# A four-layer hybrid trunk: joins of the Gated DeltaNet inverse set apart, more gates beside the norm, value products of the attention in one series, HGRN2 output transposed without TensorE

## The chip, the cores and the metric

The kernel runs on one core of a Trainium2 chip. The metric is the device time of one execution in microseconds (us), as the median of several runs. TensorE is called PE, VectorE DVE, ScalarE ACT, GpSimd POOL; SyncE (SP) issues nearly all transfers.

## The reference

Four residual layers on x of 1024 positions by D = 1024, all in fp32: HGRN2, sliding-window attention (SWA), Gated DeltaNet (GDN), HGRN2. Each is a norm with a shift and scale from a condition vector, one wide input projection, a token mixer, a product with a SiLU gate, and an output projection.

```python
x = x + gate * mixer(rmsnorm(x, g) * (1 + scale) + shift)

def hgrn2_mixer(h, w_in, w_out, onorm_g, lb):          # 8 heads of 128
    q, f_pre, i_, z = jnp.split(h @ w_in, 4, axis=-1)
    log_f = jnp.log(lb + (1.0 - lb) * jax.nn.sigmoid(f_pre))
    k = (1.0 - lb) * jax.nn.sigmoid(-f_pre)
    o = hgrn2_scan(silu(q), k, i_, log_f)              # S = diag(f) S + k v^T ; o = q S
    return (rmsnorm(o, onorm_g) * jax.nn.silu(z)) @ w_out

def swa_mixer(h, w_in, w_out, ...):                    # 16 query heads, 4 key heads of 64
    q, k, v, z = split(h @ w_in)                       # q, k: norm, then rotary
    p = softmax over the last 128 keys, with a sink per head
    return ((p @ v) * jax.nn.silu(z)) @ w_out

def gdn_mixer(h, w_in, w_out, conv_w, ...):            # 8 key heads, 16 value heads of 128
    qkv, z, a, b = split(h @ w_in)
    q, k, v = split(silu(causal_conv(qkv, conv_w)))    # 4 taps; q, k: l2norm
    # per chunk: A = beta k k^T * decay (strictly lower); X = (A + I)^-1 [v beta, k beta e^d]
    # v_new = u - w S ; o = (q e^d) S + (q k^T decay) v_new ; S = S e^dlast + k^T v_new
    return (rmsnorm(o, onorm_g) * jax.nn.silu(z)) @ w_out
```

## The kernel before

x lies feature-major, 128 features by 512 positions (a half) to a tile, in eight k blocks. The norm of a half splits its result into hhi and hlo, which together hold fp32. Weights come by SP in blocks of 256 KB (w_raw, three buffers; four k blocks by 128 columns, or two by 256), ACT splits off w_hi (L179), DVE w_lo (L180), each with four buffers. A projection column of a half is 8 k blocks by the three matmuls of mm3 (L204 to L206): hi·hi, lo·hi and hi·lo, 128 x 512 each. proj_ps, projt_ps (positions on the partitions) and outp_ps, out_ps are such products and share three banks of PSUM (two tagged proj, one ta). All else on PE is plain fp32: transposes, state products, inverses. PSUM's other tags are lev (two banks), tr, o and s (one each).

The token mixers' generators yield an estimate of how much work should come between two of their steps, and weave(...) interleaves them with the projections of the next head (or unit) in proportion to such estimates; high_priority and burst set offsets of the scheduler's priorities, tied(...) keeps a list of matmuls together behind its first, and issue_after orders an instruction behind another. A side stream of the next layers' shift and scale (ada_w, ada_acc) runs beside. The scheduler writes one instruction order for each engine from this.

- The norm: norm_stats, then norm_apply (L496), for each k block one DVE pass n_t (L504, into an SBUF tile), one ACT pass hhi (L505) and one DVE pass hlo (L506). trunk calls it for each half when the layer before has written that half. early(...) projects half 0 of the next layer beside the norm of half 1.
- HGRN2 (hgrn2, L956): 8 heads, two halves each. mix forms the intra-chunk matrix in levels j = 2, 8, 32. At j = 32 the products of L1087 go into column groups of 32 of PE's columns: per chunk of 128, 96 columns in the first, 64 in the second and 32 in the third. At a half's end the normed output (L1132, DVE, from o_ps) is transposed by PE (ot_ps, L1136, four transposes), multiplied by the gate (L1139, DVE) and, for heads 0 to 6, written to od (L1141) for the output projection; head 7 goes on in SBUF. kh_ps (L1104) are four more transposes.
- SWA (swa, L1219): for each block of 128 positions four scores, softmax, then for each of two key blocks four transposes pt_ps (L1368) and two value products pv_ps (L1374). ev_k norms and rotates k in each of four evacuations.
- GDN (gdn, L537): 8 units u. proj_kq projects k and q (conv: an ACT copy to gd_xs, three DVE passes of L650 behind the ACT pass of L648), proj_v the values, proj_z two gate columns. inverse(u) joins 32-blocks to 64 and 64 to 128 in four steps (z_ps, L811, L819 to L821, L828, L836), with copies by ACT and DVE between; scan(u) then uses it. While scan(u) runs, inverse(u + 1) and the projections listed by ZL run beside it. DVE's stream transpose of 128x512 stands at L859.

## Time and profile before

| what | value |
|---|---|
| median of 3 runs | 2690.08 us (2689.09 to 2697.81) |
| the profiled execution | 2695.95 us, its span 2694.2 us, granted clock 0.992 |
| PE busy | 2609.7 us (97%) |
| DVE busy | 2010.2 us (75%) |
| ACT busy | 1272.9 us (47%) |
| DMA | 273.29 MB |

The span runs from the first to the last instruction on the engines; the execution is 1.75 us longer. Busy PE time counts the modelled end of a matmul, so plain projection matmuls of 128x512 last 0.40 us in a row of the timeline and start every 0.23 us. The layers lie at about 62 to 640 us (HGRN2), 648 to 1122 (SWA), 1122 to 2128 (GDN) and 2128 to 2694 (HGRN2).

### The profile page before, as it was taken

Reading aid. Unit: us, or ns where it says so; the run is one execution under the profiler, and the core shown is the slowest. Engines: PE = TensorE matmul, PEld = TensorE weight load, DVE = VectorE, ACT = ScalarE, POOL = GpSimd, SP = SyncE. Lnnn points to the kernel's source line nnn. Section 1 sums busy time; section 2 is a strip of 40 time slices with the busy share of each in tenths; the row PEclk is TensorE's granted clock in tenths of the full one; section 3 lists DMA queues with packets and bytes.
Section 4 is the critical chain, followed back from the end, with each engine's and each line's share of the span. In section 5 each row is a group of like instructions: output and inputs, shape, how many; then the busy total and the mean of one; then the engine's idle time right before and its main releaser. Section 6 shows DMA issues by size and latency. Waiting matters only on the chain.

```text
span 2694.2 us, 51458 instructions
## 1 busy us (share of the span) xinstructions
PE 2609.7 (97%) x18927; PEld 2102.4 (78%) x18927; DVE 2010.2 (75%) x5619; ACT 1272.9 (47%) x3268; POOL 136.7 (5%) x352
## 2 busy tenths in 40 slices
...
GB/s 241 92 93 84 68 79 72 110 137 157 59 87 103 75 158 91 114 98 84 102 115 99 96 105 100 94 97 82 179 254 132 71 60 37 56 51 43 49 118 115
DMA packets 361490, 273.29 MB, mean 101 GB/s; under 512 B 70499, under 2 KB 294166, under 8 KB 361238
## 3 DMA queue, kind: packets, MB, share of 16 engines
...
HBM read 224.77 MB, written 45.15 MB: 100 GB/s over the span
## 4 chain that ended last, share of the span: by engine, by line
PE 71%; DVE 17%; DMA 5%; ACT 3%; issue 3%; SPq 1%; POOL 0%; DVEq 0%; ACTq 0%; POOLq 0%
PE proj_ps L206 10%; PE proj_ps L205 9%; PE proj_ps L204 9%; PE outp_ps L204 5%; PE outp_ps L205 5%; PE outp_ps L206 5%; DMA ada_w<-in_ada_w_dram 3%; PE projt_ps L204 3%; PE projt_ps L206 3%; PE projt_ps L205 3%; DVE w_lo L180 2%; DVE gd_tb L650 2%; PE pv_ps L1374 1%; DVE ada_acc L413 1%; PE w_ps L890 1%
## 5 line engine op out<-in xcount | busy, mean ns | idle before, releaser
L204 PE MATMUL proj_ps<-hhi,w_hi 128*128 128x512 f32 x1664 | 675.8, 406 | 6.1 <-ACT gd_tb L648 5.9
L206 PE MATMUL proj_ps<-hhi,w_lo 128*128 128x512 f32 x1664 | 679.9, 409 | 0.0
L205 PE MATMUL proj_ps<-hlo,w_hi 128*128 128x512 f32 x1664 | 671.2, 403 | 0.0
L204 PEld LDWEIGHTS proj_ps<-hhi,w_hi 128*128 128x128 f32 x1664 | 315.3, 190 | 59.4 <-ACT gd_tb L648 6.3
L205 PEld LDWEIGHTS proj_ps<-hlo,w_hi 128*128 128x128 f32 x1664 | 314.7, 189 | 59.0 <-issue 2.4
L206 PEld LDWEIGHTS proj_ps<-hhi,w_lo 128*128 128x128 f32 x1664 | 315.0, 189 | 56.1 <-issue 1.0
L179 ACT CAST w_hi<-w_raw 128x512 fp32r<-128x512 f32 x332 | 202.0, 611 | 303.3 <-PE proj_ps L205 188.1
L180 DVE TENSOR_TENSOR w_lo<-w_raw,w_hi 128x512 fp32r<-128x512 f32 x332 | 223.1, 674 | 155.2 <-ACT w_hi L179 129.1
L205 PE MATMUL projt_ps<-w_lo,hhi 128*128 128x256 f32 x896 | 258.7, 291 | 4.7 <-DVE w_lo L180 4.7
L204 PE MATMUL projt_ps<-w_hi,hhi 128*128 128x256 f32 x896 | 257.8, 290 | 0.6 <-ACT w_hi L179 0.6
L206 PE MATMUL projt_ps<-w_hi,hlo 128*128 128x256 f32 x896 | 256.8, 290 | 0.0
L204 PE MATMUL outp_ps<-o_hi,w_hi 128*128 128x512 f32 x576 | 229.2, 400 | 4.7 <-ACT o_hi L1200 3.4
L205 PE MATMUL outp_ps<-o_lo,w_hi 128*128 128x512 f32 x576 | 229.4, 399 | 0.0
L206 PE MATMUL outp_ps<-o_hi,w_lo 128*128 128x512 f32 x576 | 226.8, 396 | 0.7 <-DVE w_lo L183 0.7
L205 PEld LDWEIGHTS projt_ps<-w_lo,hhi 128*128 128x128 f32 x896 | 171.1, 192 | 8.1 <-DVE w_lo L180 6.0
L204 PEld LDWEIGHTS projt_ps<-w_hi,hhi 128*128 128x128 f32 x896 | 171.1, 192 | 3.7 <-ACT w_hi L179 1.0
L206 PEld LDWEIGHTS projt_ps<-w_hi,hlo 128*128 128x128 f32 x896 | 170.8, 192 | 2.4 <-issue 1.0
L650 DVE SCALAR_TENSOR_TENSOR gd_tb<-gd_xs,taps,gd_tb 128x512 f32<-128x512 f32 x192 | 145.2, 756 | 28.3 <-ACT gd_tb L648 19.7
L182 ACT ACTIVATE w_hi<-w_raw,par 128x512 fp32r<-128x512 f32 (+1 forms) x136 | 94.3, 698 | 137.0 <-PE outp_ps L205 89.2
L204 PEld LDWEIGHTS outp_ps<-o_hi,w_hi 128*128 128x128 f32 x576 | 108.8, 189 | 29.1 <-ACT o_hi L1200 4.9
L413 DVE SCALAR_TENSOR_TENSOR ada_acc<-ada_w,par,ada_acc 128x512 f32<-128x512 f32 x140 | 104.8, 749 | 33.4 <-DMA ada_w<-in_ada_w_dram 32.5
L206 PEld LDWEIGHTS outp_ps<-o_hi,w_lo 128*128 128x128 f32 x576 | 108.7, 189 | 23.5 <-DVE w_lo L183 1.3
...
## 6 DMA issues: line engine op xcount, KB each, us to landing
ada_w<-in_ada_w_dram SPq DMA_DIRECT2D x160, 256.0 KB, 2.8
w_raw<-in_hg_in_w_dram SPq DMA_DIRECT2D x136, 256.0 KB, 2.8
w_raw<-in_gd_in_w_dram SPq DMA_DIRECT2D x108, 256.0 KB, 3.0
o_in<-od SPq DMA_DIRECT2D x72, 256.0 KB, 3.2
w_raw<-in_gd_out_w_dram SPq DMA_DIRECT2D x64, 256.0 KB, 2.9
w_raw<-in_sw_in_w_dram SPq DMA_DIRECT2D x48, 256.0 KB, 2.9
w_raw<-in_hg_out_w_dram SPq DMA_DIRECT2D x40, 256.0 KB, 2.8
...
```

The lines of the kernel that those rows point to most:

```text
L179: nc.scalar.copy(hi, raw)
L180: nc.vector.tensor_tensor(lo, raw, hi.bitcast(F32), ALU.subtract)
L182: nc.scalar.activation(hi, raw, AF.Copy, scale=scale)
L204: mm(out, a[0], b[0], start=start, stop=False)
L205: mm(out, a[0], b[1], start=False, stop=False)
L206: mm(out, a[1], b[0], start=False, stop=stop)
L413: self.nc.vector.scalar_tensor_tensor(acc, w, c, acc, ALU.mult, ALU.add)
L650: nc.vector.scalar_tensor_tensor(y, xs[:, j:j + HT], w(j), y, ALU.mult, ALU.add)
L890: nc.tensor.matmul(po[:, hd[a]], dd["u"][a, hf][:, cs], rhs, start=True, stop=True)
L1374: nc.tensor.matmul(po[a * 64:(a + 1) * 64], vg[:, n + 1 - nkb + b, :], p4[:, :, a, :], start=b == 0, stop=b == nkb - 1)
```

## The change

In HGRN2, heads 0 to 6, the four PE transposes of the output go. The norm's product writes the half as blocks of 32 positions, DVE's stream transpose turns the 32x32 blocks, four DMAs of 64 KB put them into their places in a DRAM tile pd, one DMA reads the transposed half back (256 KB), and the gate product and the write to od follow at level 8 of the next half. The level-32 products become sixteen matmuls in four column groups, 64 columns in the fullest per chunk, all tied.

The norm's n_t goes to PSUM (tag lev). norm_apply is a generator, and for half 1 it is left to the next layer: HGRN2 and SWA drain it at their start; GDN drains four k blocks behind the convolution of each of its first two columns (k and q), and hold puts the next convolution's copy behind the last hhi of them.

In GDN, gates of units 1 and 2 for half 0 are projected early, beside the norm, and later gates are each done one half earlier (ZL), which loads 24 more weight blocks. The four steps of an inverse's joins are issued after the last projection matmul emitted before them (apart) and yield 2200 each. In SWA the value products of a block form one series behind all its transposes; k's evacuations go in pairs with one 16-wide rsqrt; and the order at the start is v and q for half 0 early, then v, k, z, q.

```diff
-NB = {"n_acc": 1, "n_sq": 2, "n_t": 2}
+NB = {"n_acc": 1, "n_sq": 2}
-ZL = ((2, 0, 1),), ((3, 0, 1),), ((4, 0, 1),), ((5, 0, 1),), ((6, 0),), ((6, 1),), ((7, 0, 1),), ()
+ZL = ((2, 1), (3, 0)), ((3, 1), (4, 0)), ((4, 1), (5, 0)), ((5, 1), (6, 0)), ((6, 1),), ((7, 0),), ((7, 1),), ()
...
+    def apart(self, mms):
+
+        with self.tc.issue_after(self.mm.ins):
+            self.tied(mms)
...
-        mm(out, a[1], b[0], start=False, stop=stop)
+        self.mm = mm(out, a[1], b[0], start=False, stop=stop)
...
     def norm_apply(self, i, hf, rb):
+
         nc = self.nc
...
-            t = self.np.tile([P, HT], F32, name="n_t", tag="n_t", bufs=NB["n_t"])
+            t = self.psum("lev", "n_t", 2)
             G, S = self.gcol[:, i, k:k + 1], self.shift(i, k)
             nc.vector.scalar_tensor_tensor(t, x[:, k, :], G, rb, ALU.mult, ALU.mult)
-            nc.scalar.activation(hhi[:, k, :], t, AF.Identity, bias=S)
+            self.piece = nc.scalar.activation(hhi[:, k, :], t, AF.Identity, bias=S)
             nc.vector.scalar_tensor_tensor(hlo[:, k, :], t, S, hhi[:, k, :].bitcast(F32), ALU.add, ALU.subtract)
+            yield 1
...
-            nc.scalar.copy(xs[:, 3:], ps)
+            with self.tc.issue_after(self.hold.ins) if self.hold else nullcontext():
+                nc.scalar.copy(xs[:, 3:], ps)
...
             for j in (2, 1, 0):
-                nc.vector.scalar_tensor_tensor(y, xs[:, j:j + HT], w(j), y, ALU.mult, ALU.add)
+                last = nc.vector.scalar_tensor_tensor(y, xs[:, j:j + HT], w(j), y, ALU.mult, ALU.add)
+
+            self.piece = None
+            with self.tc.issue_after(last.ins):
+                drain(take(self.last, self.parts))
+            self.hold = self.piece
...
-            yield 900
+            yield 2200
             za, zb = bank("z_ps", 32), bank("z_ps", 32)
-            self.tied([f for g in range(N) for f in (
+            self.apart([f for g in range(N) for f in (
...
-        self.early(proj_kq(0, ds[0], ((0,),)), EV)
+        self.parts = 4
+        self.early(chain(proj_kq(0, ds[0], ((0,),)), proj_z(1, ds[1], (0,)), proj_z(2, ds[2], (0,))), EV)
+        drain(self.last)
         self.spill_x(1)
         decays()
         drain(proj_kq(0, ds[0], ((1,),)))
-        weave(self.tc, (inverse(0, ds[0]), 28000, 0, 0.8, 100),
-              (chain(proj_z(0, ds[0], (1,)), proj_v(0, ds[0]), proj_z(1, ds[1]), proj_kq(1, ds[1])), 72800, 0, 1, 0))
+        weave(self.tc, (inverse(0, ds[0]), 34300, 0, 0.85, 100),
+              (chain(proj_z(0, ds[0], (1,)), proj_v(0, ds[0]), proj_z(1, ds[1], (1,)), proj_kq(1, ds[1])), 62400, 0, 1, 0))
...
-        bufs = {"X": 1, "q": 3, "f": 3, "kg": 3, "qf": 3, "tmp": 3, "v": 3, "zs": 3, "kht": 1, "k0": 2}
+        bufs = {"X": 1, "q": 3, "f": 3, "kg": 3, "qf": 3, "tmp": 3, "v": 3, "zs": 4, "kht": 1, "k0": 2}
...
+        def gate():
+
+            h, hf, z = pend.pop()
+            rows = (slice(h * P, (h + 1) * P), slice(hf * HT, (hf + 1) * HT))
+            t = tl("tmp")
+            nc.sync.dma_start(t, self.pd[rows])
+            nc.vector.tensor_tensor(v4(z, "c b"), v4(t, "b c"), v4(z, "c b"), ALU.mult)
+            nc.sync.dma_start(od[rows], z)
...
-                        with self.burst():
-                          for c in range(NC):
-                            for g in range(3):
-                                gs = slice(g * 32, (g + 1) * 32)
-                                nc.tensor.matmul(pl[gs, c, g + 1:, :], kg[:, c * P + g * 32:c * P + (g + 1) * 32], xv[:, c, g::3 if g == 0 else 4 - g, :][:, :3 - g, :] if g < 2 else xv[:, c, 2:3, :], start=True, stop=True)
...
+                        def mm(c, k, g, x, b):
+                            return nc.tensor.matmul(pl[g * 32:(g + 1) * 32, c, b], kg[:, c * P + k * 32:c * P + (k + 1) * 32], xv[:, c, x, :], start=True, stop=True)
+
+                        self.tied([lambda c=c, m=m: mm(c, *m) for c in range(NC) for m in (
+                            (0, 3, slice(6, 7), slice(3, 4)), (0, 0, slice(0, 4, 3), slice(1, 3)),
+                            (1, 1, slice(1, 5, 3), slice(2, 4)), (2, 2, slice(2, 3), slice(3, 4)))])
...
+                    if l == 3 and pend:
+                        gate()
...
-                on = tl("tmp")
-                nc.vector.tensor_tensor(on.rearrange("p (c t) -> p c t", c=NC), po.rearrange("p (c t) -> p c t", c=NC), r[:, :, None].to_broadcast([P, NC, P]), ALU.mult)
-                pt = self.psum("tr", "ot_ps", 1)
-                for c in range(NC):
-                    cs = slice(c * P, (c + 1) * P)
-                    nc.tensor.transpose(pt[:, cs], on[:, cs], self.ident)
-                yield 436
-                of = tl("tmp")
-                nc.vector.tensor_tensor(of, pt, d["zs", hf], ALU.mult)
                 if h < HA:
-                    nc.sync.dma_start(od[h * P:(h + 1) * P, hf * HT:(hf + 1) * HT], of)
+
+
+                    nc.vector.tensor_tensor(v4(on, "b c"), v4(po, "c b"), r[:, :, None, None].to_broadcast([P, NC, 4, 32]), ALU.mult)
+                    ob = tl("tmp")
+                    nc.vector.transpose(ob, on)
+                    dst = self.pd[h * P:(h + 1) * P, hf * HT:(hf + 1) * HT].rearrange("(b q) (a t) -> a q b t", b=4, a=4)
+                    for a in range(4):
+                        nc.sync.dma_start(dst[a], ob[a * 32:(a + 1) * 32].rearrange("q (b t) -> q b t", b=4))
+                    pend.append((h, hf, d["zs", hf]))
...
-                    for a in range(2):
-                        nc.tensor.matmul(po[a * 64:(a + 1) * 64], vg[:, n + 1 - nkb + b, :], p4[:, :, a, :], start=b == 0, stop=b == nkb - 1)
-                        yield 430
...
+                self.tied([lambda b=b, a=a: nc.tensor.matmul(po[a * 64:(a + 1) * 64], vg[:, n + 1 - nkb + b, :], p4s[b][:, :, a, :], start=b == nkb - 1, stop=b == 0)
+                           for b in reversed(range(nkb)) for a in range(2)])
+                yield 860 * nkb
...
-        self.early(kv(0))
+        ds = [dict(q=[None, None], zs=[None, None], rq=[None, None]) for _ in range(G)]
+        drain(self.last)
+        self.early(chain(proj_v(0), proj_q(0, ds[0], (0, 1))))
         self.spill_x(1)
-        drain(kv(1))
-        ds = [dict() for _ in range(G)]
-        drain(proj(0, ds[0]))
+        drain(proj_v(1))
+        drain(self.proj_tm(self.load_tm(w_in, 1024), ev_k))
+        drain(chain(proj_z(0, ds[0]), proj_q(0, ds[0], (2, 3))))
...
-                k.norm(nxt, hf)
+                a = k.norm_apply(nxt, hf, k.norm_stats(hf))
...
+                    k.last = a
```

Three places show how the order moves. The line numbers of the changed kernel differ: w_lo is L187 there, the projections' matmuls L211 to L213, the convolution L657.

The first is DVE's order at the end of head 0, half 0, in the first HGRN2 layer. Before:

```order
L1003 TENSOR_TENSOR hg_zs<-proj_ps,hg_tmp 128x512
L162 TENSOR_TENSOR rs_t<-rs_t,rs_y 128x4
L163 SCALAR_TENSOR_TENSOR rs_y<-rs_t,rs_y 128x4
L1132 TENSOR_TENSOR hg_tmp<-o_ps,rs_y 128x512
L180 TENSOR_TENSOR w_lo<-w_raw,w_hi 128x512 x2
L1139 TENSOR_TENSOR hg_tmp<-ot_ps,hg_zs 128x512
L411 TENSOR_SCALAR ada_acc<-ada_w,par 128x512
```

After the change, in the same place:

```order
L1161 TENSOR_TENSOR hg_tmp<-o_ps,rs_y 128x4x4x32
L1015 TENSOR_TENSOR hg_zs<-proj_ps,hg_tmp 128x512
L1163 STREAM_TRANSPOSE hg_tmp<-hg_tmp 128x512
L1151 SCALAR_TENSOR_TENSOR hg_S<-hg_S,hg_F,s_ps 128x128
L187 TENSOR_TENSOR w_lo<-w_raw,w_hi 128x512 x2
L418 TENSOR_SCALAR ada_acc<-ada_w,par 128x512
L988 TENSOR_TENSOR hg_q<-proj_ps,hg_tmp 128x16x32
L420 SCALAR_TENSOR_TENSOR ada_acc<-ada_w,par,ada_acc 128x512 x3
L1047 TENSOR_TENSOR hg_zs<-hg_tmp,hg_zs 128x512
```

The gate product (L1139, now L1047) stood two w_lo behind the norm's product; now eight instructions stand between it and the stream transpose.

The second is PE's order at the last two join steps of the last inverse (unit 7), each 16 matmuls on 64x64. Before, with the tiles' numbers:

```order
L821 MATMUL z_ps_22227<-gd_Z_12713,gd_Uc_22058 32x32
L205 MATMUL proj_ps_22128<-hlo_12658,w_hi_22014 128x512
L206 MATMUL proj_ps_22128<-hhi_12657,w_lo_22015 128x512
L658 MATMUL vtr_ps_22003<-ident_85,gd_tb_21991 128x128 x4
L204 MATMUL proj_ps_22128<-hhi_12657,w_hi_22014 128x512
L828 MATMUL z_ps_22286<-gd_Z_12713,gd_uq_21405 64x64 x16
...
L205 MATMUL proj_ps_22128<-hlo_12658,w_hi_22014 128x512
L836 MATMUL z_ps_22329<-gd_uq_21405,gd_Z_12713 64x64 x16
```

After the change:

```order
L831 MATMUL z_ps_22335<-gd_Z_12740,gd_Uc_22188 32x32
L838 MATMUL z_ps_22433<-gd_Z_12740,gd_uq_21668 64x64 x16
L211 MATMUL outp_ps_22620<-o_hi_22562,w_hi_22622 128x512
L211 MATMUL outp_ps_22687<-o_hi_22562,w_hi_22689 128x512
L846 MATMUL z_ps_22506<-gd_uq_21668,gd_Z_12740 64x64 x16
L212 MATMUL outp_ps_22620<-o_lo_22563,w_hi_22622 128x512
```

Three projection matmuls and a transpose group, and then seven projection matmuls, stood in the two gaps; now nothing and two matmuls of the output projection stand there.

The third is DVE's order at the start of GDN, with the second half's norm (n_t, hlo) and the first convolutions (gd_tb<-gd_xs). Before:

```order
L506 SCALAR_TENSOR_TENSOR hlo<-n_t,mod,hhi 128x512 x2
L504 SCALAR_TENSOR_TENSOR n_t<-x_11280,gcol,n_rb 128x512 x2
L180 TENSOR_TENSOR w_lo<-w_raw,w_hi 128x512
L506 SCALAR_TENSOR_TENSOR hlo<-n_t,mod,hhi 128x512 x2
L650 SCALAR_TENSOR_TENSOR gd_tb<-gd_xs,taps,gd_tb 128x512 x2
L556 TENSOR_TENSOR gd_wab<-w_raw,gd_wab 128x8x32
L650 SCALAR_TENSOR_TENSOR gd_tb<-gd_xs,taps,gd_tb 128x512
L652 SCALAR_TENSOR_TENSOR gd_k<-gd_tb 128x512
```

After the change, from behind the first of the three steps of q's convolution on:

```order
L187 TENSOR_TENSOR w_lo<-w_raw,w_hi 128x512
L657 SCALAR_TENSOR_TENSOR gd_tb<-gd_xs,taps,gd_tb 128x512
L187 TENSOR_TENSOR w_lo<-w_raw,w_hi 128x512
L657 SCALAR_TENSOR_TENSOR gd_tb<-gd_xs,taps,gd_tb 128x512
L509 SCALAR_TENSOR_TENSOR n_t<-x_11341,gcol,n_rb 128x512 x2
L664 SCALAR_TENSOR_TENSOR gd_q<-gd_tb 128x512
L511 SCALAR_TENSOR_TENSOR hlo<-n_t,mod,hhi 128x512 x2
L509 SCALAR_TENSOR_TENSOR n_t<-x_11341,gcol,n_rb 128x512 x2
L739 SCALAR_TENSOR_TENSOR gd_tb<-gd_tb,proj_ps 128x512
L511 SCALAR_TENSOR_TENSOR hlo<-n_t,mod,hhi 128x512 x2
L739 SCALAR_TENSOR_TENSOR gd_tb<-gd_tb,proj_ps 128x512
L187 TENSOR_TENSOR w_lo<-w_raw,w_hi 128x512 x6
```

Before, the whole norm of the half stood ahead of the first convolution; now one half of it stands behind k's convolution and the other behind q's. Ahead of the rows shown stand the three steps of k's convolution, two n_t, gd_k, two hlo, two n_t, one w_lo, two hlo and the first step of q's.

## Rows read from the trace of the kernel before

**Rows 1.** The page: each engine's busy time; the chain by engine.
```profile
PE 2609.7 (97%) x18927; PEld 2102.4 (78%) x18927; DVE 2010.2 (75%) x5619; ACT 1272.9 (47%) x3268; POOL 136.7 (5%) x352
...
PE 71%; DVE 17%; DMA 5%; ACT 3%; issue 3%; SPq 1%; POOL 0%; DVEq 0%; ACTq 0%; POOLq 0%
```

**Rows 2.** What PE waited for: us in total, times, longest us.
```profile
PE lev_ps L1040 <- DVE hg_X L1063: 6.8, 19, 1.8
PE z_ps L828 <- DVE gd_uq L823: 6.6, 7, 1.6
PE proj_ps L204 <- ACT gd_tb L648: 5.9, 1, 5.9
PE ot_ps L1136 <- DVE hg_tmp L1132: 5.6, 11, 1.3
PE projt_ps L205 <- DVE w_lo L180: 4.7, 5, 1.4
...
PE ab_ps L575 <- DVE gd_tb L727: 2.0, 1, 2.0
```

**Rows 3.** Windows of HGRN2 (first), GDN, HGRN2 (last); the first row names the columns.
```profile
core 0: us, PE busy (x) PEld busy (x) DVE busy (x) ACT busy (x) POOL busy (x), PEclk, DMA share, GB/s
62.00:640.00 578.00, 560.15 (x4763) 461.35 (x4762) 412.80 (x1193) 216.63 (x488) 32.40 (x69) 0.99 0.32 95
1122.00:2128.00 1006.00, 978.51 (x6286) 783.99 (x6287) 833.33 (x2178) 574.11 (x1664) 69.23 (x171) 0.99 0.42 115
2128.00:2694.00 566.00, 551.65 (x4743) 456.85 (x4742) 355.79 (x1091) 205.42 (x467) 29.37 (x64) 1.00 0.21 64
```

**Rows 4.** Timeline of PE in the first HGRN2 layer: start, length, what.
```profile
246.67 0.40 PE L206 MATMUL proj_ps<-hhi,w_lo 128*128 128x512 f32 x1
246.90 0.40 PE L204 MATMUL proj_ps<-hhi,w_hi 128*128 128x512 f32 x1
247.14 0.60 PE L1104 MATMUL kh_ps<-ident,hg_kg 128*128 128x128 f32 x4
247.50 0.48 PE L205 MATMUL proj_ps<-hlo,w_hi 128*128 128x512 f32 x1
247.81 0.39 PE L206 MATMUL proj_ps<-hhi,w_lo 128*128 128x512 f32 x1
```

**Rows 5.** Lines on tile hg_tmp: duration ns min/median/max, first and last start.
```profile
L1139 DVE TENSOR_TENSOR hg_tmp<-ot_ps,hg_zs x32: 673/684/692, 128.7 to 2632.1; 128x512 f32<-128x512 f32 x32
```

**Rows 6.** Lines on tile gd_of in GDN, same columns.
```profile
L859 DVE STREAM_TRANSPOSE gd_of<-gd_of x32: 689/704/712, 1304.5 to 1983.9; 128x512 f32<-128x512 f32 x32
```

**Rows 7.** The page's DMA issues: count, KB each, median us from issue to landing.
```profile
od<-gd_of SPq DMA_DIRECT2D x128, 64.0 KB, 1.8
o_z<-zd SPq DMA_DIRECT2D x32, 256.0 KB, 3.7
```

**Rows 8.** The page's groups of instructions: busy us, mean ns; idle before.
```profile
L180 DVE TENSOR_TENSOR w_lo<-w_raw,w_hi 128x512 fp32r<-128x512 f32 x332 | 223.1, 674 | 155.2 <-ACT w_hi L179 129.1
```

**Rows 9.** Timeline of PE in the first HGRN2 layer: two groups of level products.
```profile
153.92 0.55 PE L1040 MATMUL lev_ps<-hg_X,hg_kg 128*32 128x48 f32 x32 [0.28 <-DVE hg_X L1063]
...
157.34 0.85 PE L1087 MATMUL lev_ps<-hg_X,hg_kg 128*32 128x96 f32 x24
```

**Rows 10.** Timeline of PE at the start of SWA: two waits.
```profile
661.16 0.39 PE L205 MATMUL projt_ps<-w_lo,hhi 128*128 128x256 f32 x1 [1.43 <-DVE w_lo L180]
...
663.51 0.58 PE L205 MATMUL projt_ps<-w_lo,hhi 128*128 128x256 f32 x1 [1.37 <-DVE w_lo L180]
```

**Rows 11.** Timeline of DVE at the start of GDN.
```profile
1123.07 1.41 DVE L504 SCALAR_TENSOR_TENSOR n_t<-x,gcol,n_rb 128x512 f32<-128x512 f32 x2 [1.28 <-PE n_rb L493]
...
1135.96 1.41 DVE L506 SCALAR_TENSOR_TENSOR hlo<-n_t,mod,hhi 128x512 fp32r<-128x512 f32 x2
1137.36 1.69 DVE L650 SCALAR_TENSOR_TENSOR gd_tb<-gd_xs,taps,gd_tb 128x512 f32<-128x512 f32 x2
```

**Rows 12.** A window at the start of GDN, columns as in rows 3.
```profile
1137.00:1141.30 4.30, 3.99 (x9) 2.82 (x9) 3.57 (x6) 1.88 (x5) 2.47 (x9) 0.50 0.42 98
```

120 lines of the change are left out of this document (68 added, 52 removed).

## The prediction

> **What bounds the kernel now.** I read the page's busy line first, then the chain that ended last, then the list of what TensorE waits for, and then the places that the change touches. TensorE (PE) is busy 2609.7 us, 97% of the span, and the chain runs through it for 71% [rows 1]. So the idle time of PE in all is only 2694.2 − 2609.7 = 84.5 us, and a change has two ways to gain: PE work taken out, or some of these 84.5 us. The waits list says that the idle time is scattered: the largest entries are 5.6 to 6.8 us in 1 to 19 pieces [rows 2]. The stage table says how much room VectorE (DVE) has as PE's feeder: it is busy 412.8 of 578 us in the first HGRN2 layer, 355.8 of 566 in the last, but 833.3 of 1006 in Gated DeltaNet (GDN) [rows 3]. Work moved from PE to DVE has cover in HGRN2 and little in GDN.
>
> **Output transposes of HGRN2.** 28 groups of four PE transposes (heads 0 to 6, two halves, two layers) go. Their price comes from the same four transposes of kh_ps, alone between projection matmuls: from the matmul before (246.90) to the second one after (247.81) is 0.91 us, where two plain steps of 0.23 (as 246.67 to 246.90) take 0.46; net 0.45 [rows 4]. 28 × 0.45 = −12.6. Of that some 0.17 is the change from the projections' split matmuls to plain fp32 ones and back, since the step after such a group is 0.31 and not 0.23 (247.50 to 247.81), and I take the same 0.08 for going in; where the group stood beside another of its kind these 0.17 stay, so the smaller bound is 28 × 0.28 = −8. Beside it stands PE's wait on L1132 ahead of them, 5.6 us in 11 pieces [rows 2]; 28 of 32 groups go, so −4.9.
>
> What replaces them is DVE work and DMAs. Each half-head had L1132 and the gate product of L1139 (0.68 [rows 5]) on DVE; it now has L1132 in another order, a stream transpose (0.70 at L859, same shape [rows 6]) and a gate product that I price as L1139: +0.70 × 28 = +19.7 us of DVE over the two HGRN2 layers. DVE is idle 578 − 412.8 + 566 − 355.8 = 375 us there [rows 3], so I cost it at nothing; if DVE were the feeder at that moment it would cost up to 0.7 each. Four 64 KB writes (1.8 us to landing, as od<-gd_of) and one 256 KB read (3.7, as o_z<-zd) follow one another [rows 7]: 5.5 us from transpose to gate product. In the order of the first head DVE has between the two a small state update and seven instructions of 128x512, two w_lo, four ada_acc and q, at 0.68 each [rows 5, 8] 4.8 us. So the gate product would stand some 0.7 us ahead of its data: 28 × 0.7 = 20 us of DVE waiting. PE's projections would not feel it, since a w_lo holds four k blocks, twelve matmuls of 0.23 for a half, and there are four buffers; what feels it is the next half's chain of level products, whose waits for hg_X are 6.8 us now [rows 2]. I take +2, with bounds of 0 and of 28 × 5.5 = 154. The SyncE queue gets 28 × 5 more issues, and what stands behind one that waits is weight loads, which run ahead by three raw buffers; that is in the same +2.
>
> The Trainium skill, "VectorE: DVE Perf Modes", section "Rules for kernel authors", says to do a 128×128 transpose on TensorE where PSUM is an acceptable destination, since DVE transposes 32×32 blocks only. By that rule the old form was the right one, and the sum would be without these two terms, 17.5 us higher. The trace speaks for the move all the same, since the engine that the rule wants to load is the one at 97% and DVE has the room.
>
> **Products at level j = 32.** Twelve matmuls with up to 96 columns in one column group become sixteen, with 64 in the fullest. The group with 96 takes 0.85 us, a group of the 48-column form 0.55 [rows 9]. Linear in the columns of the fullest group, 64 gives 0.55 + 16/48 × 0.30 = 0.65: −0.20 for each of 32 groups, −6.4. If what counts is the number of matmuls, 16 against 12, it is 0.85 × 16/12, +0.28 each, +9; the 48-column group holds 16 as well (32 records, two to a matmul) and takes 0.55, so I take the columns. ScalarE (ACT) makes 32 more copies, at no cost: it is busy for 47% of the span [rows 1].
>
> **Sliding-window attention (SWA).** The value products stood in 57 places of PE's order and stand in 32. A place saved is worth the two changes of kind, 0.17 [rows 4]; between 7 places that lie between projections (1.2 us) and all 25 (4.2), I take −2.5. At the layer's start PE waits for w_lo at 661.16 and 663.51, 2.8 us in sum [rows 10], while DVE works at the norm's second half. With v and q ahead of k's long evacuation, I take −3, these two waits, between 0 and −6.
>
> **Start of GDN.** This is the biggest hole. The second half's norm holds DVE from 1123.07 to 1137.36, the first convolution waits behind it (L650 begins when it ends [rows 11]), and PE waits 5.9 us for a bank, and another 2.0 for ab_ps [rows 2]. After that hole the granted clock is 0.50 from 1137 to 1141.3, the lower of its two levels (1.2 GHz): nine matmuls at 0.44 where 0.23 is usual [rows 4, 12], 1.9 us. Together 9.8 us. In the new order the convolution goes first, and six columns of gates for half 0, of 24 matmuls each, stand behind k and q where two stood. I walk it from the end of k's projection, with 0.70 for each DVE pass of 128x512 [rows 8, 11]. Two ACT passes (taken at 0.7 as well) and 15 of DVE later, at 11.9, the w_lo of the second gate column is there (the first row of the new order in the third place shown above); PE has had 50 projection matmuls and a transpose group, 50 × 0.23 + 0.45 = 11.9, and does not wait. Six passes on, q is ready at 16.1, when PE has done 18 more and waits 0.1. Then PE wants a bank that the gate's product frees, 11 passes after 11.9, at 19.6, and is there at 17.9: 1.7. Two matmuls on it wants the first w_lo of the row of six, 15 passes after 11.9, at 22.4, and is there at 20.1: 2.3. That makes 4.1 us in pieces instead of 9.8, a gain of 5.7 if no piece brings the slow clock. I take −5, between −10 (all of it) and +1 (each pass of the norm late by a wait for its bank, which it now shares with the level tag).
>
> **The rest of GDN.** 24 more loads: 24 × 0.67 = +16.1 us of DVE, in a layer where it is at 83% [rows 3, 8]. Eight of them fall at the start and are counted there; the others lie beside PE's work. Cost 0, up to +16 where DVE is the feeder. The joins: PE waits 6.6 us in 7 pieces at L828 [rows 2]. Counted in projection matmuls of 0.23 us, the gaps between an inverse's steps held 0.9 to 2.5 us of other work; the new order puts 3.5 to 5.0 us there for inverses 2 to 6, 1.1 to 1.8 for 0 and 1, and next to none for inverse 7, since the gates that filled it were done at the start (the second place shown above). Five of seven waits go, −4.7, and the last inverse gets two or three bare waits for a pair of DVE copies, 2 × 0.68 each at the price of [rows 5], +3.5. Net −1. The norm's scratch in PSUM instead of SBUF changes no count; 0.
>
> **Sum.** −12.6 − 4.9 + 2 − 6.4 − 2.5 − 3 − 5 − 1 = −33.4 us. The profiled execution took 2695.95 us, 1.75 above its span and 5.9 above the median of 2690.08, so the same change to a typical run gives 2690.1 − 33.4 = 2656.7 us (2662.5 by the profiled one). I forecast **2657 us**.
>
> **Rivals.** A measurement of this kernel can tell about 0.3%, 8 us, from no change.
>
> *More comes than I count (2640).* The start of GDN closes (5 more), the waits at lev_ps for hg_X go as well (−6.8 [rows 2]), and SWA reaches −4.2 and −6 where I took −2.5 and −3: 2657 − 5 − 6.8 − 4.7 = 2640. For it: each of these waits is caused by DVE arriving late by under 2 us. Against: DVE gets more to do in every one of these places.
>
> *GDN takes it back (2681).* DVE's +16.1 us shows on PE in full, its start gains nothing, and the last inverse loses 3 more: 2657 + 16 + 5 + 3 = 2681. For it: 83% over the layer is a mean, and stretches lie above it. Against: PE's waits for w_lo are 4.7 us in all [rows 2], and the two largest are at the start of SWA [rows 10].
>
> *The change does not do what it says (2688).* The joins are no further apart where it matters (inverses 0 and 1 keep their gaps, 7 loses its), the start of GDN stalls as before, and the transposes were covered: then only the columns term is left, less the new waits, −4 or so (2686 to 2690). Against: on an engine at 97% hardly any work is covered.
>
> *Slower (2706).* The round trip through DRAM holds DVE. The gate product stands in DVE's order ahead of the state updates and level passes of the next half; when its read lands late these are late, and PE, which takes its instructions in order, stands at lev_ps or s_ps. It decides from (33.4 + 8)/28 = 1.5 us of PE wait for each gate; at 1.75 us, 28 × 1.75 − 33.4 = +16, 2706. For it: 5.5 us of transfer against 4.8 us of cover, and SyncE may hold the read behind an ada load. Against: the read is only some 0.7 us late by these rows.
>
> **How the numbers follow.** Forecast 0.55 (own range 2646 to 2670), more 0.17, GDN takes back 0.15, no effect 0.06, slower 0.07. Faster by over 0.3% means under 2682: the forecast, the second, and two thirds of the third, 0.82. Within 0.3% is 2682 to 2698: the rest of the third and the fourth, 0.11. Slower 0.07. The range 2632 to 2686 holds the first three cases but for their ends, and leaves out the slow one and most of the fourth.
>
> **What the new profile would show.** Right: PE busy down by 20 to 25 us and its idle time by about 10; ot_ps left with 16 transposes; the level group at 0.65 us; no wait for hg_tmp at the gate product longer than 1 us on DVE; at the start of GDN two waits of 1.7 and 2.3 us, for a gate product's bank and for w_lo, in place of the one of 5.9, and no slow clock behind them; waits at z_ps gone but for the last inverse. Wrong: waits of PE on lev_ps and s_ps in HGRN2 with DVE waiting for hg_tmp<-pd ahead of them; a level group of 0.85 us or more; PE idle in GDN up by 10 us or more with DVE full.

## The result, and the profile after

The changed kernel takes 2699.53 us (median of 16 runs, 2695.29 to 2705.34); the kernel before took 2690.68 us beside it (16 runs). The ratio is 1.0032, 95% interval [1.0021, 1.0043]: **8.9 us slower**, where 33 us of gain were forecast. The profiled execution took 2700.09 us, with a span of 2698.4 us.

The page's busy line and chain by engine, to be read beside [rows 1]:

```profile
PE 2590.7 (96%) x19071; PEld 2092.7 (78%) x19071; DVE 2031.8 (75%) x5649; ACT 1284.9 (48%) x3324; POOL 137.3 (5%) x352
...
PE 69%; DVE 17%; DMA 6%; ACT 5%; issue 2%; SPq 1%; POOL 0%; DVEq 0%; ACTq 0%; POOLq 0%
```

PE is busy for 19.0 us less, near the 21.5 that the sum counted as work (12.6 + 6.4 + 2.5). But its idle time, 84.5 us before, is 2698.4 − 2590.7 = 107.7 us: 23.2 more, where 10 less was expected. So work did go, and waits took its place. By layers (from a layer's first n_rb matmul to the next layer's, in the two profiles) HGRN2's two take 15.8 us less together, SWA 0.4 more, and GDN 19.9 more (1047.8, 1027.9 before): the loss lies in GDN. What PE waited for (us in total, times, longest us), beside [rows 2]:

```profile
PE vtr_ps L670 <- DVE gd_tb L664: 12.5, 8, 7.2
PE lev_ps L1064 <- DVE hg_X L1087: 7.9, 16, 1.2
PE z_ps L820 <- ACT gd_Tc L805: 5.0, 1, 5.0
PE proj_ps L213 <- DVE w_lo L187: 4.8, 3, 2.2
...
PE o_ps L1141 <- DVE hg_tmp L1161: 3.8, 10, 0.9
PE proj_ps L211 <- ACT gd_tb L655: 3.7, 4, 1.8
PE z_ps L838 <- DVE gd_uq L833: 2.2, 2, 1.7
```

The waits the change aimed at have shrunk: that of z_ps for gd_uq from 6.6 to 2.2 us, and the one of 5.9 at the start of GDN is gone (the 3.7 us on gd_tb L655 lie further on, the longest, 1.8, at 1752; what stands at the start now is shown below). The two new ones, 7.2 and 5.0 us in one piece each, stand at one place, ahead of the last inverse. The timeline of all engines there:

```profile
1906.87 0.63 PE L670 MATMUL vtr_ps<-ident,gd_tb 128*128 128x128 f32 x4
1907.26 0.48 PE L213 MATMUL proj_ps<-hhi,w_lo 128*128 128x512 f32 x1
...
1909.14 0.60 ACT L651 COPY gd_xs<-proj_ps 128x512 f32<-128x512 f32 x1
...
1909.45 8.87 SPq L804 DMA_DIRECT2D gd_tmp<-tblk  x8
...
1912.20 0.75 DVE L657 SCALAR_TENSOR_TENSOR gd_tb<-gd_xs,taps,gd_tb 128x512 f32<-128x512 f32 x1
...
1914.22 0.65 DVE L664 SCALAR_TENSOR_TENSOR gd_tb<-gd_tb 128x512 f32<-128x512 f32 x1
...
1914.93 1.12 PE L670 MATMUL vtr_ps<-ident,gd_tb 128*128 128x128 f32 x4 [7.19 <-DVE gd_tb L664]
...
1920.34 0.65 ACT L805 COPY gd_Tc<-gd_tmp 128x512 f32<-128x512 f32 x1 [3.11 <-DMA od<-gd_of]
...
1921.04 1.92 PE L820 MATMUL z_ps<-gd_Tc,gd_uq 32*32 32x32 f32 x64 [4.99 <-ACT gd_Tc L805]
...
1923.87 0.23 PE L829 MATMUL z_ps<-gd_Uc,gd_Z 32*32 32x32 f32 x1 [0.92 <-DVE gd_Z L823]
...
1927.13 1.97 PE L838 MATMUL z_ps<-gd_Z,gd_uq 64*64 64x64 f32 x32 [0.77 <-ACT gd_Z L832]
...
1930.58 1.98 PE L846 MATMUL z_ps<-gd_uq,gd_Z 64*64 64x64 f32 x32 [0.33 <-DVE gd_Z L843]
```

and in the kernel before:

```profile
1894.04 4.04 SPq L792 DMA_DIRECT2D gd_tmp<-tblk  x8
...
1903.76 1.20 PE L811 MATMUL z_ps<-gd_Tc,gd_uq 32*32 32x32 f32 x64
```

At 1907.26 PE issues the last projection matmul that it has ahead of the joins. Next in its order are v's transposes, which wait for the whole convolution of that matmul's bank (ACT's copy, DVE's taps, the gate L664). Then come the joins, which wait for the diagonal blocks that go out to DRAM and back (tblk, read from 1909.45 on). In the kernel before projections stood between these steps. The windows of this stretch, first before and then after (columns as in [rows 3]):

```profile
1910.00:1920.00 10.00, 9.77 (x101) 7.59 (x101) 7.46 (x13) 7.35 (x19) 0.00 (x0) 1.00 0.36 101
1920.00:1930.00 10.00, 6.34 (x30) 4.28 (x29) 7.08 (x17) 7.44 (x28) 0.00 (x0) 0.99 0.45 149
```

```profile
1910.00:1920.00 10.00, 1.12 (x4) 0.71 (x4) 5.34 (x13) 2.10 (x6) 0.00 (x0) 0.60 0.80 225
1920.00:1930.00 10.00, 6.99 (x194) 6.08 (x194) 5.03 (x8) 3.26 (x6) 3.61 (x6) 0.50 0.66 202
1930.00:1940.00 10.00, 9.67 (x62) 7.79 (x62) 5.47 (x12) 3.55 (x10) 0.00 (x0) 0.71 0.48 140
```

PE works 1.1 of 10 us, and then the joins and the work behind them run at a granted clock of 0.50 (the lower level, 1.2 GHz): the 64 records of L820 take 1.92 us, and the same in the kernel before (L811) 1.20.

### The profile page after: what moved, and what is told of

Its sections match the earlier page's. It is cut to its first block, busy times and chain, and to the rows that moved or that the text cites. A ratio compares the mean times of both kernels' runs of the same rounds, so it can differ in the third digit from the quotient of the medians.

```text
span 2698.4 us, 52166 instructions
## 1 busy us (share of the span) xinstructions
PE 2590.7 (96%) x19071; PEld 2092.7 (78%) x19071; DVE 2031.8 (75%) x5649; ACT 1284.9 (48%) x3324; POOL 137.3 (5%) x352
## 3 DMA queue, kind: packets, MB, share of 16 engines
q0 software_dynamic: 288, 1.05, 0.1%
## 4 chain that ended last, share of the span: by engine, by line
PE 69%; DVE 17%; DMA 6%; ACT 5%; issue 2%; SPq 1%; POOL 0%; DVEq 0%; ACTq 0%; POOLq 0%
PE proj_ps L212 9%; PE proj_ps L213 9%; PE proj_ps L211 9%; PE outp_ps L213 5%; PE outp_ps L212 5%; PE outp_ps L211 5%; PE projt_ps L212 3%; PE projt_ps L211 3%; PE projt_ps L213 3%; DMA ada_w<-in_ada_w_dram 2%; DVE w_lo L187 2%; DVE gd_tb L657 1%; PE pv_ps L1418 1%; PE ada_row L407 1%; PE w_ps L900 1%
## 5 line engine op out<-in xcount | busy, mean ns | idle before, releaser
L211 PE MATMUL proj_ps<-hhi,w_hi 128*128 128x512 f32 x1664 | 674.4, 405 | 5.6 <-ACT gd_tb L655 3.7
L213 PE MATMUL proj_ps<-hhi,w_lo 128*128 128x512 f32 x1664 | 674.6, 406 | 4.8 <-DVE w_lo L187 4.8
L211 PEld LDWEIGHTS proj_ps<-hhi,w_hi 128*128 128x128 f32 x1664 | 314.6, 189 | 63.9 <-ACT gd_tb L655 6.2
L213 PEld LDWEIGHTS proj_ps<-hhi,w_lo 128*128 128x128 f32 x1664 | 314.4, 189 | 63.4 <-DVE w_lo L187 6.3
L186 ACT CAST w_hi<-w_raw 128x512 fp32r<-128x512 f32 x356 | 217.4, 612 | 305.6 <-PE proj_ps L212 181.0
L187 DVE TENSOR_TENSOR w_lo<-w_raw,w_hi 128x512 fp32r<-128x512 f32 x356 | 239.2, 675 | 140.4 <-ACT w_hi L186 138.3
L211 PE MATMUL projt_ps<-w_hi,hhi 128*128 128x256 f32 x896 | 256.1, 290 | 1.4 <-ACT w_hi L186 1.4
L213 PE MATMUL projt_ps<-w_hi,hlo 128*128 128x256 f32 x896 | 255.2, 289 | 0.0
L211 PE MATMUL outp_ps<-o_hi,w_hi 128*128 128x512 f32 x576 | 231.3, 405 | 6.7 <-ACT o_hi L1235 3.2
L213 PE MATMUL outp_ps<-o_hi,w_lo 128*128 128x512 f32 x576 | 231.6, 404 | 5.8 <-DVE w_lo L190 4.4
L211 PEld LDWEIGHTS projt_ps<-w_hi,hhi 128*128 128x128 f32 x896 | 169.7, 191 | 4.9 <-ACT w_hi L186 2.0
L213 PEld LDWEIGHTS projt_ps<-w_hi,hlo 128*128 128x128 f32 x896 | 169.7, 191 | 2.3 <-issue 1.4
L657 DVE SCALAR_TENSOR_TENSOR gd_tb<-gd_xs,taps,gd_tb 128x512 f32<-128x512 f32 x192 | 144.4, 752 | 10.5 <-ACT gd_tb L655 7.3
L211 PEld LDWEIGHTS outp_ps<-o_hi,w_hi 128*128 128x128 f32 x576 | 110.1, 192 | 32.3 <-ACT o_hi L1235 5.4
L213 PEld LDWEIGHTS outp_ps<-o_hi,w_lo 128*128 128x128 f32 x576 | 110.2, 192 | 28.8 <-DVE w_lo L190 5.3
L212 PEld LDWEIGHTS outp_ps<-o_lo,w_hi 128*128 128x128 f32 x576 | 110.5, 192 | 24.0 <-DVE o_lo L1236 1.4
```

The costliest lines, as they stand in the source:

```text
L186: nc.scalar.copy(hi, raw)
L187: nc.vector.tensor_tensor(lo, raw, hi.bitcast(F32), ALU.subtract)
L211: mm(out, a[0], b[0], start=start, stop=False)
L212: mm(out, a[0], b[1], start=False, stop=False)
L213: self.mm = mm(out, a[1], b[0], start=False, stop=stop)
L657: last = nc.vector.scalar_tensor_tensor(y, xs[:, j:j + HT], w(j), y, ALU.mult, ALU.add)
```

## Experiments

The change is taken apart into six parts: **gates** (four gate columns projected at GDN's start, and the table ZL of what is woven into each stretch), **joins**, **norm** (the second half's norm spread), **attention** (SWA's order and value products), **level** (products at j = 32) and **output** (HGRN2's output path). A ratio is to the kernel before, run on the same chip, and differences between kernels are taken from the ratios, 0.0010 being 2.7 us; "alone" means before plus one part, "without" means the changed kernel less one.

### Which part is slow

**e1**, without gates:

```diff
-ZL = ((2, 1), (3, 0)), ((3, 1), (4, 0)), ((4, 1), (5, 0)), ((5, 1), (6, 0)), ((6, 1),), ((7, 0),), ((7, 1),), ()
+ZL = ((2, 0, 1),), ((3, 0, 1),), ((4, 0, 1),), ((5, 0, 1),), ((6, 0),), ((6, 1),), ((7, 0, 1),), ()
...
-        self.early(chain(proj_kq(0, ds[0], ((0,),)), proj_z(1, ds[1], (0,)), proj_z(2, ds[2], (0,))), EV)
+        self.early(proj_kq(0, ds[0], ((0,),)), EV)
```

> The changed kernel with its gates part alone undone (early projects k, q and the gates of unit 0 only, the list ZL as before; joins, norm, HGRN2 and attention stay changed). Theory A (the gates moved to the layer's start leave nothing to run beside the last unit's values and inverse, PE stands there for 12 us and then runs at the lower clock): the hole at the last inverse goes and the time falls by 15 to 20 us, to 2680 to 2685 us, if the start of the layer loses nothing. Theory B (the joins set apart hold the last inverse back): the hole stays, 2695 to 2700. Theory C (24 more weight blocks load DVE everywhere in the layer): some 8 us better in many small pieces, 2690, with the hole still there.

Measured: 2680.00 us, ratio 0.9956 [0.9943, 0.9970]. **e2**, gates alone, is the same diff the other way round on the kernel before:

```diff
-        self.early(proj_kq(0, ds[0], ((0,),)), EV)
+        self.early(chain(proj_kq(0, ds[0], ((0,),)), proj_z(1, ds[1], (0,)), proj_z(2, ds[2], (0,))), EV)
```

> The kernel before with the gates part alone (two gate columns each of units 1 and 2 for half 0 early, ZL shifted). Theory A: a hole of 10 us or more in front of the last inverse and a slow clock behind it, +12 to +18 us, 2703 to 2709. Theory B: about as before, 2691. Theory C: +8 in small pieces, 2699.

Measured: 2709.57 us, 1.0069 [1.0057, 1.0082], +18.5 us. The gates part costs 18.5 us by itself and 20.5 (1.0032 against 0.9956) in company. **e3**, output and level alone, and **e4**, the changed kernel with another table:

```diff
+                    nc.vector.transpose(ob, on)
...
+                        self.tied([lambda c=c, m=m: mm(c, *m) for c in range(NC) for m in (
```

> The kernel before with the HGRN2 part alone (stream transpose and DRAM round trip for the output, sixteen products at level 32). The stage tables of the two kernels give the first layer 10 us shorter and the last 6 us: if that is the part's own doing 2674 us. If the deferred norm and not this part brought it, 2685 or more. If the round trip costs PE anything, over 2691.

Measured: 2683.48 us, 0.9974 [0.9964, 0.9985], −7.

```diff
-ZL = ((2, 1), (3, 0)), ((3, 1), (4, 0)), ((4, 1), (5, 0)), ((5, 1), (6, 0)), ((6, 1),), ((7, 0),), ((7, 1),), ()
+ZL = ((2, 1),), ((3, 0, 1),), ((4, 0, 1),), ((5, 0, 1),), ((6, 0),), ((6, 1),), ((7, 0, 1),), ()
```

> The changed kernel with one edit to the list ZL: both early gate halves stay early, but the later gates keep their old places, so that unit 0's stretch has two gate columns where it had four and the stretch beside the last inverse has four again. Theory A: the hole in front of the last inverse goes, 2681 to 2686, minus what unit 0's stretch loses by its missing work (0 to 6 us). Theory B and C: 2695 to 2700, the hole stays.

Measured: 2697.25 us, 1.0025 [1.0015, 1.0034]. The stretch ahead of the last inverse has 48 projection matmuls more and neither of the two long waits is left (2.28 and 1.48 us stand between the join's steps); but the first stretch has that many fewer, and PE's timeline shows waits there that were not in the changed kernel:

```profile
1339.38 0.49 PE L916 MATMUL w_ps<-gd_wg,gd_uq 128*128 128x128 f32 x2 [1.29 <-ACT gd_wg L915]
...
1347.74 0.51 PE L211 MATMUL proj_ps<-hhi,w_hi 128*128 128x512 f32 x1 [1.34 <-ACT gd_tb L655]
...
1354.98 0.66 PE L670 MATMUL vtr_ps<-ident,gd_tb 128*128 128x128 f32 x4 [1.50 <-DVE gd_tb L664]
...
1371.23 1.15 PE L838 MATMUL z_ps<-gd_Z,gd_uq 64*64 64x64 f32 x32 [1.09 <-DVE gd_uq L833]
```

By its time e4 lies in the range of the other two theories, by its trace it bears out the first, whose 0 to 6 us for the first stretch were too few. The hole moves with the missing work.

### Is it want of other work?

**e11** puts the gap into the third stretch; **e13** leaves the order as changed and projects unit 7's second half of gates twice, 48 matmuls (10.9 us of PE) whose result is written over by the same values:

```diff
-ZL = ((2, 1), (3, 0)), ((3, 1), (4, 0)), ((4, 1), (5, 0)), ((5, 1), (6, 0)), ((6, 1),), ((7, 0),), ((7, 1),), ()
+ZL = ((2, 1), (3, 0)), ((3, 1), (4, 0)), ((4, 1),), ((5, 0, 1),), ((6, 0),), ((6, 1),), ((7, 0, 1),), ()
```

> The changed kernel with the two missing gate columns taken from unit 2's stretch instead of the last inverse's (the list ZL shifted up to there, and as before behind it). Theory A as first put (only the last stretch can't spare its fill, since no scan of a later unit stands there): 2682 to 2686. Theory A in the form that the run with the gap at unit 0 suggests (every stretch needs its fill, and what is done at the start is done where VectorE and not TensorE is the limit): 2693 to 2699, with the hole at unit 2.

Measured: 2688.02 us, 0.9980 [0.9971, 0.9989], between the two ranges; 14 us faster than the changed kernel, 12 faster than e4, 6.5 slower than e1. e11 differs from e1 at the layer's start and in the third stretch, and the profiles tell the two apart: the first inverse's joins begin 226.4 us into the layer in e11 and 194.0 in e1, with 102 projection matmuls more ahead of them, 23.5 us at 0.23. The 8.9 us left are nearly all of the 9.1 by which e11's whole layer is longer. So the gap in the third stretch costs nothing that can be seen, and the difference is the start.

```diff
-ZL = ((2, 1), (3, 0)), ((3, 1), (4, 0)), ((4, 1), (5, 0)), ((5, 1), (6, 0)), ((6, 1),), ((7, 0),), ((7, 1),), ()
+ZL = ((2, 1), (3, 0)), ((3, 1), (4, 0)), ((4, 1), (5, 0)), ((5, 1), (6, 0)), ((6, 1),), ((7, 0),), ((7, 1), (7, 1)), ()
```

> The changed kernel with the two gate columns of unit 7, half 1, projected twice, so that the stretch beside the last inverse has four columns again; the second time is work that computes nothing new (48 matmuls, 10.9 us of TensorE). If the hole there is for want of other work (theory A), the added 10.9 us cost nothing or less, since they fill a hole of 12 us and keep the clock up: 2690 to 2700. If TensorE's time there is set by the amount of work, 2710.

Measured: 2696.93 us, 1.0018 [1.0009, 1.0027]. 10.9 us of work more, and the kernel takes no longer for it (3.8 us shorter, with intervals that overlap). The windows of e13 at the last inverse:

```profile
1910.00:1920.00 10.00, 9.92 (x195) 7.95 (x194) 9.20 (x25) 5.63 (x16) 4.11 (x6) 1.00 0.66 219
1920.00:1930.00 10.00, 8.15 (x90) 5.99 (x89) 7.09 (x12) 6.00 (x14) 1.40 (x3) 1.00 0.65 169
1930.00:1940.00 10.00, 6.95 (x32) 4.67 (x33) 8.45 (x19) 7.98 (x27) 0.00 (x0) 1.00 0.44 141
```

The stretch is full and the clock stays at 1.00. This settles the end of GDN: the hole is want of other work.

### The other parts

**e5**, attention alone; **e6**, joins alone; **e7**, norm alone:

```diff
+        self.early(chain(proj_v(0), proj_q(0, ds[0], (0, 1))))
...
+                self.tied([lambda b=b, a=a: nc.tensor.matmul(po[a * 64:(a + 1) * 64], vg[:, n + 1 - nkb + b, :], p4s[b][:, :, a, :], start=b == nkb - 1, stop=b == 0)
```

> The kernel before with the attention part alone (value products in one series, k's evacuations in pairs, v and q first). The prediction's two terms for it are -2.5 and -3: 2685 us. The stage table of the changed kernel shows the attention's stretch as long as before (465.9 against 465.5 us between the norms of its two ends): by that reading, no gain, 2690.

Measured: 2689.10 us, 0.9989 [0.9981, 0.9998], −3.

```diff
-            yield 900
+            yield 2200
...
-            self.tied([lambda g=g, q=q: nc.tensor.matmul(z[q, g % 8, :], uv[lo, g, up], Z[lo, g, :], start=True, stop=True)
+            self.apart([lambda g=g, q=q: nc.tensor.matmul(z[q, g % 8, :], uv[lo, g, up], Z[lo, g, :], start=True, stop=True)
```

> The kernel before with the joins part alone (the four steps issued after the last projection matmul emitted ahead of them, longer yields); the gates stay where they were, so the last inverse keeps its projections. If the joins are what they were priced at, the waits at z_ps shrink by 4 to 5 us and nothing else moves: 2686. If the joins delay the scans that wait for the inverse: 2692 to 2698.

Measured: 2689.59 us, 0.9992 [0.9983, 1.0000], −2.

```diff
-            t = self.np.tile([P, HT], F32, name="n_t", tag="n_t", bufs=NB["n_t"])
+            t = self.psum("lev", "n_t", 2)
...
+                drain(take(self.last, self.parts))
```

> The kernel before with the norm part alone (second half's norm behind the first convolutions, n_t in PSUM). The wait of 5.9 us at the start of the Gated DeltaNet layer and the slow clock behind it go, 5 to 10 us: 2681 to 2686. If the pieces only move the wait: 2690.

Measured: 2694.09 us, 1.0012 [1.0002, 1.0022], +3. In its profile GDN (from the layer's first n_rb matmul to the next layer's) takes 1019.8 us, 1027.9 before: the hole at its start is gone as predicted. But SWA takes 475.2, 465.5 before. DVE's timeline of e7 at its start, and then PE's:

```profile
652.46 1.41 DVE L509 SCALAR_TENSOR_TENSOR n_t<-x,gcol,n_rb 128x512 f32<-128x512 f32 x2
...
662.24 1.40 DVE L509 SCALAR_TENSOR_TENSOR n_t<-x,gcol,n_rb 128x512 f32<-128x512 f32 x2
663.55 0.68 DVE L187 TENSOR_TENSOR w_lo<-w_raw,w_hi 128x512 fp32r<-128x512 f32 x1
```

```profile
664.29 0.39 PE L212 MATMUL projt_ps<-w_lo,hhi 128*128 128x256 f32 x1 [2.06 <-DVE w_lo L187]
...
689.05 0.39 PE L212 MATMUL projt_ps<-w_lo,hhi 128*128 128x256 f32 x1 [2.85 <-DVE w_lo L187]
```

The norm's second half stands in one piece, 11 us without a w_lo, where two w_lo stood between its passes before: that is the first of the two waits. The second (0.88 in the kernel before, at 684.46) comes over 20 us behind the norm, among the evacuations of k, and its cause isn't shown. In the changed kernel, with v and q first, five w_lo stand between the passes, both waits are gone, and the longest left there is 1.06 (at 656.32, for w_hi). SWA as a whole still takes 5 us more with the norm part than without: 465.9 in the changed kernel and 466.1 in e1, 460.9 in e12. **e8**, without gates and attention, and **e12**, without gates and norm, ask what each is worth beside the rest:

```diff
-        self.early(chain(proj_v(0), proj_q(0, ds[0], (0, 1))))
+        self.early(kv(0))
```

> The changed kernel without the gates and without the attention part (norm, joins and HGRN2 stay). Against e1_no_gates, which measured 2680.0, it gives the attention part once more in the other surroundings: 2680 if it is worth nothing, 2685 if it is worth its price, below 2680 if it costs.

Measured: 2688.56 us, 0.9984 [0.9976, 0.9993]; against e1 the attention part is worth 8 us beside the spread norm, 3 alone.

```diff
-            t = self.psum("lev", "n_t", 2)
+            t = self.np.tile([P, HT], F32, name="n_t", tag="n_t", bufs=NB["n_t"])
```

> The changed kernel without the gates and without the norm part (joins, HGRN2, attention). The parts alone measured -7.8, -1.9 and -2.4 us, the norm alone +2.6: by their sum 2679, about 2 us below e1_no_gates, whose 2680.0 has the norm part. If the new order at the start of the attention needs the norm to be spread, 2682 or more.

Measured: 2680.79 us, 0.9954 [0.9941, 0.9966], as e1. So spreading the norm brings nothing in this company (GDN is 7.9 us shorter in e1's profile than in e12's, SWA 5.2 and HGRN2 2.9 longer), and e1 and e12 are the fastest versions here, 12 us below before and 21 below the changed kernel.

### HGRN2's output

**e9**, level alone; **e10**, output alone; **e14**, the kernel before with the transposing left out for heads 0 to 6 and nothing in its place (the gate multiplies the untransposed product):

```diff
+                        self.tied([lambda c=c, m=m: mm(c, *m) for c in range(NC) for m in (
+                            (0, 3, slice(6, 7), slice(3, 4)), (0, 0, slice(0, 4, 3), slice(1, 3)),
```

> The kernel before with the level-32 products alone changed (sixteen matmuls in four column groups). In the changed kernel a group of them takes 0.58 us from its start to the next projection matmul where it took 0.78: 32 x 0.20 = 6.4 us, 2685 us. If the time of a group is covered by other waits, 2689 to 2691.

Measured: 2688.69 us, 0.9985 [0.9976, 0.9994], −4.

```diff
+                    nc.vector.transpose(ob, on)
...
+                    pend.append((h, hf, d["zs", hf]))
```

> The kernel before with the output of HGRN2 alone changed (stream transpose and round trip through DRAM, no transposes on TensorE for heads 0 to 6). The prediction's terms: -12.6 for the transposes, -4.9 for their waits, +2 for new ones, 2676 us. The whole HGRN2 part measured -7.8, so if the level products are worth their 6.4, what is left is about -1.5: 2690.

Measured: 2693.90 us, 1.0003 [0.9995, 1.0012], no gain.

```diff
+                pt = on
+                if h == HA:
+                    pt = self.psum("tr", "ot_ps", 1)
```

> The kernel before without any transpose of the HGRN2 output for heads 0 to 6: the gate's product takes the untransposed tile, so the output of these heads is not the reference's; no stream transpose, no round trip, VectorE's passes as before. Theory P (TensorE's 112 transposes lay in time in which it would else wait for VectorE's chain of level products): 2687 to 2692. Theory Q (they cost their 12.6 us and 4.9 of waits, and the stream transposes and gate products in VectorE's queue took it back by delaying that chain): 2674 to 2679.

Measured: 2685.16 us, 0.9975 [0.9965, 0.9986], −6.7, between the two theories. Even with nothing in their place the transposes were worth 6.7 us to the kernel and not 17.5. The page's busy line and PE's waits in e10:

```profile
PE 2596.7 (96%) x18815; PEld 2090.0 (78%) x18815; DVE 2023.2 (75%) x5647; ACT 1272.9 (47%) x3268; POOL 137.7 (5%) x352
```

```profile
PE lev_ps L1059 <- DVE hg_X L1082: 10.8, 18, 2.2
...
PE o_ps L1135 <- DVE hg_tmp L1155: 4.7, 10, 1.5
...
PE o_ps L1136 <- POOL hg_at L1100: 2.2, 1, 2.2
```

PE's busy time fell by 13.0 us, near the 12.6 of the sum (busy time isn't work alone, though: e14, with as many PE records, is at 2590.3, and e15 below, with as many as the kernel before, at 2603.6); its idle time rose from 84.5 to 2696.1 − 2596.7 = 99.4. The wait at ot_ps (5.6) is gone, and lev_ps for hg_X rose from 6.8 to 10.8 (11.0 in e14), o_ps for the norm product from 1.7 to 4.7 (1.3 in e14). PE comes earlier to products that the mix's DVE chain delivers no earlier.

By layers, in single profiles: HGRN2's two take 1162.2 us in e14 and 1172.8 in e10, 1173.4 to 1177.6 in four kernels whose HGRN2 is unchanged (before, e2, e5, e6). GDN, with the same order on each engine as before (1027.9), takes 1032.1 in e14 and 1036.6 in e10. So in their own layers the transposes were worth 11 to 15 us, what replaces them gives most of that back there, and some more is lost in a layer that the edit doesn't touch; the last section returns to it.

What takes e10's remaining 7 us over e14? **e15** adds 28 stream transposes to the kernel before, **e17** puts e10's gate product later, **e18** takes e10's round trip away (the product is gated at once, straight from the stream transpose):

```diff
+                if h < HA:
+                    nc.vector.transpose(of, on)
```

> The kernel before with 28 stream transposes of 128x512 added on VectorE ahead of the gate's product (their result is overwritten), TensorE's transposes kept. Theory Q: VectorE's 0.70 us more for each half-head delay the chain and show on TensorE, 2696 to 2708. Theory P: TensorE keeps its pace but for a part, 2690 to 2695.

Measured: 2691.98 us, 0.9997 [0.9986, 1.0007].

```diff
-                    if l == 3 and pend:
-                        gate()
...
                 nc.scalar.copy(kht, pt)
+                if pend:
+                    gate()
```

> The kernel before with the output part of HGRN2 alone (e10_output_only, which measured +0.8), and the late gate product moved from level 8 of the next half to behind that half's kh transposes, out of the chain of level passes. If the gate product's place in VectorE's chain is what takes back the gain, 2684 to 2687; if it is not, 2691 to 2695.

Measured: 2697.10 us, 1.0017 [1.0007, 1.0026], above both ranges.

```diff
-                    for a in range(4):
-                        nc.sync.dma_start(dst[a], ob[a * 32:(a + 1) * 32].rearrange("q (b t) -> q b t", b=4))
-                    pend.append((h, hf, d["zs", hf]))
+                    z = d["zs", hf]
+                    nc.vector.tensor_tensor(v4(z, "c b"), v4(ob, "b c"), v4(z, "c b"), ALU.mult)
```

> e10_output_only without the round trip: the stream transpose stays, the gate's product follows it at once on the blocks as they lie, and no block goes to DRAM and back, so the output of heads 0 to 6 is not the reference's. VectorE's passes are those of e10_output_only. If the round trip or the delayed product takes back the gain, 2684 to 2687, as without any transpose (e14_no_transpose, 0.9975 of before); if VectorE's added pass and its strided writes take it, 2690 to 2694.

Measured: 2693.59 us, 1.0006 [0.9997, 1.0014]. So neither the round trip nor the gate's place is the cause. By its range e18 speaks for DVE's added pass and its strided writes. The writes are no slower: the norm's product in blocks of 32 takes 0.69 us in e18 (L1155) as in the kernel before (L1132). The added pass costs nothing where PE still transposes (e15); in an order without PE's transposes no run takes it out. It, or what the scheduler moved with it, is left, and the cause stays open. **e16** asks whether the part is worth anything in company: e12 without it.

```diff
-                    nc.vector.transpose(ob, on)
...
-                    pend.append((h, hf, d["zs", hf]))
```

> The kernel before with joins, level-32 products and attention, without gates, norm and the output part. By the sum of the parts alone (-1.9, -4.0, -2.4) 2683 to 2684; e12_no_gates_no_norm, the same with the output part, measured 2680.8. If the output part is worth nothing anywhere, 2681.

Measured: 2685.24 us, 0.9978 [0.9967, 0.9988], where e12 has 0.9954: about 6.5 us beside joins, level and attention, none alone. The runs don't say why it differs.

## Why the prediction was wrong, step by step

**The step that failed** is in "The rest of GDN": "the last inverse gets two or three bare waits for a pair of DVE copies, 2 × 0.68 each", +3.5, together with the gates' loads at 0. Those waits came to 2.0 us (0.92, 0.77 and 0.33 at the last inverse): what was left out stood ahead of them. The gates part costs 18.5 us alone (e2) and 20.5 in company (e1), in two places.

- *The end, 14 us* (e11 against the changed kernel). I looked only at the gaps between the join's steps. The same gates had also covered what leads to the join: the convolution of v's last half, 7.2 us from its bank to its transposes with nothing else in PE's order, and the diagonal blocks' trip through DRAM, which left 5.0. That trip was 1891.99 (first write) to 1901.51 (ACT's copy) in the kernel before, 9.5 us, and is 1906.20 to 1920.34, 14.1 us, now; SyncE needs 8.87 us to issue its eight reads, 4.04 before, and the DMA share in this stretch is 0.80; why the trip is longer no run shows. With the refill of e13 the trip is 11.7 us (1903.18 to 1914.89), and covered. Behind the hole the low clock stretches what follows. With work put back the hole and the low clock are gone, and the 10.9 us of that work don't lengthen the kernel (e13).
- *The start, some 6.5 us* (e11 against e1). Here the walk was near in its pieces. PE's timeline of the changed kernel, beside [rows 11, 12]:

```profile
1128.34 0.50 PE L213 MATMUL proj_ps<-hhi,w_lo 128*128 128x512 f32 x1 [1.57 <-DVE w_lo L187]
...
1131.94 0.50 PE L213 MATMUL proj_ps<-hhi,w_lo 128*128 128x512 f32 x1 [1.05 <-DVE w_lo L187]
...
1139.39 0.50 PE L211 MATMUL proj_ps<-hhi,w_hi 128*128 128x512 f32 x1 [1.23 <-DVE gd_tb L739]
...
1142.28 0.50 PE L213 MATMUL proj_ps<-hhi,w_lo 128*128 128x512 f32 x1 [2.16 <-DVE w_lo L187]
```

The gate's bank (1.7 predicted) and w_lo behind it (2.3) are there with 1.23 and 2.16, and no slow clock follows; the first two waits I had not found. 6.0 us in pieces instead of 9.8. But that is the gain of the norm part; without the gates (e1) the only wait of over 1 us in these 50 us is one of 1.50. The four columns are 96 matmuls, 22 us, of work that would have filled stretches further on and here stands where DVE must deliver its w_lo first. The prediction's sign for "GDN takes it back", PE idle in GDN up by 10 us or more with DVE full, came by half: PE's idle time there is 18.5 us up, but DVE is busy for only 5.3 of 10 us in the hole.

**Start of GDN (−5):** right in its own layer, where e7's GDN is 8.1 us shorter. What the norm part costs in SWA, 9.7 us in e7 and some 5 in the changed kernel, had no term in the sum.

**Transposes and their waits (−17.5):** the sum took freed PE time for shorter time, and what replaces the transposes for nearly free. e14 gives −6.7, e10 with what stands in their place +0.8; in HGRN2's own layers e14 is 11 to 15 us shorter, e10 1 to 5. Of the missing 11 to 16 us, 4 each are seen at lev_ps, 3 more at o_ps in e10, and some 4 at stops that the last section shows; the rest stays open.

**Level (−6.4):** right by place and row, 0.65 us a group as worked out; the timeline of the changed kernel, beside [rows 9]:

```profile
118.69 0.65 PE L1109 MATMUL lev_ps<-hg_X,hg_kg 128*32 128x32 f32 x32
```

e9 measures −4, with −6.5 to −1.6 in its interval. **Attention (−5.5):** −3 [−5.1, −0.5] alone, 8 beside the spread norm; SWA itself is 5.7 us shorter in e5's profile, near the term, and in the changed kernel the norm part takes that back. **Joins (−4.7 of the net −1):** in the changed kernel the waits at z_ps for gd_uq fell by 4.4 us as counted; joins alone (e6) change the time by 2 [−4.6, 0]. **New waits (+2):** no cost shown. The gate product waits 3.0 us for its read in six places on DVE, 0.8 at most, and taking the round trip away changes nothing (e18). The Trainium skill's rule in "VectorE: DVE Perf Modes", "Rules for kernel authors", transposes of 128×128 on TensorE, would have kept the old form, 17.5 us higher in my sum; alone the measurement sides with it only in so far as the move brings nothing (1.0003), and beside joins, level and attention the move is worth 6.5 us (e16 against e12).

Alone the parts give −7 (e3), −3, −2, +3 and +18.5, +9.5 in sum, and the whole is +8.9. That the two are so near is in part chance: in company attention is worth 8 and not 3, the norm part nothing and not +3, the gates 20.5 and not 18.5, the output 6.5 and not nothing. Of the rivals, "GDN takes it back" had the place right and the mechanism wrong: not DVE's 16 us, but fill taken from the last inverse. "Slower" had the sign right and the mechanism wrong.
